# A hybrid decoder layer on one core: the main expert stage written out as a pipeline, and more gathered rows in an earlier stage

## The chip, the cores and the metric

The kernel runs on one core of one Trainium2 chip. The metric is the device time of one execution in microseconds (us), input and output in HBM included. All data are fp32; some of the matrix products take operands of type fp32r, each split in a high part and a remainder.

## The reference

One decoder layer for 512 tokens of width 1024. A token sublayer (retention and forgetting attention, gated and merged) is followed by a channel sublayer, which is what the change is mostly about: a retrieval over 16,384 experts of one neuron each (128 x 128 product keys), plus a gated embedding.

```python
def decoder_layer(x, p):                                   # 512 x 1024
    h = layer_norm(x)
    rq, rk, rv, rg, fq, fk, fv, ff, gr, gf = split(h @ w_in)
    y_ret = (silu(rg) * group_norm(retention(rotary(rq), rotary(rk), rv))) @ w_ret_o
    y_fox = forgetting_attention(fq, fk, fv, log_sigmoid(ff + b_forget)) @ w_fox_o
    merged = sigmoid(gr + b0) * y_ret + sigmoid(gf + b1) * y_fox
    h = layer_norm(ALPHA * h + merged @ w_out)
    ple = sigmoid(h @ w_ple_gate + b) * (p @ w_ple)
    return layer_norm(ALPHA * h + peer(h) + ple)

def peer(h):                                               # 8 heads, 16 experts per token and head
    s, idx = top_k(einsum('nhcd,hckd->nhck', h @ w_q, sub_keys), 16)
    top_s, eid = top_k(all 256 sums of a head's two lists, 16)
    act = gelu(einsum('nhkd,nd->nhk', expert_u[eid], h)) * softmax(top_s)
    return einsum('nhk,nhkd->nd', act, expert_v[eid])
```

## The kernel before

The 512 tokens are two pairs of 128-token blocks, `FIRST` and `REST`. Everything up to the experts is done for `FIRST`, then for `REST`; the experts of the two pairs are computed in two different ways, side by side.

**The first pair's experts are gathered, row by row** (`Gather`). A token has 8 x 16 = 128 experts, and so has a block 128 columns: for one column, `fetch` (L869) issues on POOL an indirect DMA that brings one row of `peer_u` or `peer_v`, 1024 numbers, for each of the 128 tokens into one row buffer. `up` (L875) then multiplies it with the tokens on the DVE, with a sum; `down` (L885) adds it, weighted, to the residual `h0`. A block is 128 ups, one gelu, 128 downs; two blocks make 512 such rows. They wait in a queue, `k.feed.items`. The queue is asked for work by `k.tick`, once for each weight load of a projection, and hands out `rate` items per call, which is set by stage: 1, then 2.25 in `last_blocks` (the second pair's attention and output projections, "the second pair's first stage", 56 weight loads), 0.5 in the second pair's product keys and embedding gate, 0.75 in `spread`. What is left by the main stage is spread evenly over its blocks by `pace`.

**The second pair's experts are computed densely** (`Experts`), all 128 groups ("blocks" of the main stage) of 128 experts each. `up` is the up half of a block: 8 matmuls in the code, 16 in the trace (L799), of a `ur` tile, loaded for two blocks at once, with the tokens `h1`, and a gelu (L801) that gives `a`. `load` takes `vr`, also two blocks at once, and splits it in a high and a low fp32r part, `vh` on ACT (L196) and `vl` on the DVE (L197). `gated` multiplies `a` with the retrieval's gates `gw` on the DVE (L824; `gw` is loaded for four blocks at once) and splits the product in `ah` (ACT) and `al` (DVE). `down` is the down half: 12 matmuls (L837 to L839), `ah`·`vh`, `ah`·`vl` and `al`·`vh` for two token blocks and two halves of the width, summed over all 128 blocks in four PSUM banks `acc`. 40 up halves (`lead`) are done in `spread`, while the gates are scattered into `gd`, and four (`RES`) just ahead of the main stage's first down half, with the banks of `acc` as their target.

**Order.** The kernel is written against a tile scheduler, which places the instructions of every engine by its own timeline. From `spread` on (`in_order`) it does so for PE, ACT and the SP queue alone; DVE and POOL there keep the order in which the program emits them. In the main stage that order is, for each block: load of the next block, an up half, gate and split of the next block, the down half, then `pace` rows. Buffers: two each of `vr`, `vh`, `vl`, `gw`, `ah`, `al` (the pool `dp` has `bufs=2`); the rows go round over 8 buffers (`near`), 4 more in `dp` (`far`) and one in slot `S2`.

`Borrow` lends some tags of the first pair's product keys a place in another pool; three tags share the LG buffers of tag `lg`, `sc` (the scores that leave the PSUM tile `sp`, L642 and L645) among them. Other lines that are named below: L454 the swish product `z`, L530 the retention's product with its branch gate (`sgr`), L475 the residual that ends the second pair's first stage, L217 a weight load (`wr`).

## Time and profile before

| | |
|---|---|
| time, median of 3 runs (lowest to highest) | 1914.91 us (1912.94 to 1918.87) |
| the profiled execution: its time, its span | 1914.95 us, 1913.2 us |
| PE (matmul) busy | 1708.9 us, 89% |
| PE weight loads | 1375.3 us, 72%, beside the matmuls |
| DVE busy | 1362.5 us, 71% |
| POOL busy | 719.0 us, 38% |
| ACT busy | 610.8 us, 32% |
| DMA | 553.92 MB, mean 290 GB/s over the span |

The shares are means over a program with very different parts. In order of time: the first pair's attention and product keys (to about 444 us), the second pair's first stage (to about 752), its product keys, embedding gate and `spread` (to about 1090), the main stage (to about 1863) and the tail. The main stage has two parts: while there are up halves left to do, to about 1649 us, and after that with down halves alone. The DMA row of the page's table by slices shows the same parts: it lies above 300 GB/s from about 430 to 670 us and from 910 to 1815.

### The profile page before, as it was taken

How to read it: one execution, taken by the hardware profiler on the slowest of the kernel's cores; microseconds unless marked ns; L12 is line 12 of the kernel's file. 1: busy time of each engine (PE TensorE's matmuls, PEld its weight loads, DVE VectorE, ACT ScalarE, POOL GpSimd, SP SyncE). 2: the span in 40 equal slices, each digit the busy share in tenths (PEclk: the TensorE clock that was granted, in tenths of full speed). 3: DMA queues.
4: the chain of work that ended last, by engine and by line, in shares of the span. 5: the costliest groups of instructions: out<-in, count | busy, mean ns of one | idle time of the engine just before them, and what ended most of it. 6: DMA issues, size and time to landing. Idle time of an engine off the chain costs nothing.

```text
span 1913.2 us, 22617 instructions
## 1 busy us (share of the span) xinstructions
PE 1708.9 (89%) x7996; PEld 1375.3 (72%) x7996; DVE 1362.5 (71%) x2625; ACT 610.8 (32%) x1130; POOL 719.0 (38%) x523
## 2 busy tenths in 40 slices
PE   6999999997999898999999699999999999766664
PEld 6889888755777474877989588777888878544443
DVE  7543563699877733588979377877877778888885
ACT  4556542121133210114668322232222222222221
POOL 1000000028756720011334355555656555665630
PEclk9999999998999899999999899999999999987887
DMA  7433454459999974565888899999999999999971
GB/s 232 158 122 128 143 191 149 148 206 372 400 322 328 395 282 156 190 209 169 336 331 326 347 380 405 381 370 373 396 398 383 400 387 396 349 347 334 328 258 56
DMA packets 164674, 553.92 MB, mean 290 GB/s; under 512 B 18768, under 2 KB 52560, under 8 KB 147152
## 3 DMA queue, kind: packets, MB, share of 16 engines
q1 hardware_dynamic: 90832, 284.00, 40.9%
q0 software_dynamic: 73728, 268.47, 37.4%
q8 instruction: 63, 1.03, 0.2%
q14 instruction: 51, 0.42, 0.1%
HBM read 533.54 MB, written 18.87 MB: 289 GB/s over the span
## 4 chain that ended last, share of the span: by engine, by line
issue 41%; PE 25%; POOL 15%; DVE 10%; DMA 7%; ACT 2%; SPq 0%; POOLq 0%; DVEq 0%; ACTq 0%
POOL row L869 14%; PE pj L249 10%; PE pj L252 4%; PE hid L799 3%; DMA row<-in_peer_u,geu 3%; DVE h L885 2%; DMA row<-in_peer_v,geu 1%; PE gp L771 1%; DVE oa L762 1%; DVE ob L763 1%; DVE row L875 1%; PE ry L325 1%; PE lg L408 1%; PE sp L642 1%; DMA h<-in_x 1%
## 5 line engine op out<-in xcount | busy, mean ns | idle before, releaser
L869 POOL DMA_INDIRECT row<-in_peer_v,geu x256 | 351.4, 1373 | 509.9 <-DVE h L885 337.5
L869 POOL DMA_INDIRECT row<-in_peer_u,geu x256 | 355.7, 1389 | 329.1 <-DVE row L875 124.4
L799 PE MATMUL hid<-h1f,ur 128*128 128x256 f32 x1984 | 444.0, 380 | 3.7 <-DMA ur<-in_uT 3.7
L799 PEld LDWEIGHTS hid<-h1f,ur 128*128 128x128 f32 x1984 | 375.7, 191 | 57.7 <-DMA ur<-in_uT 3.9
L837 PE MATMUL acc<-vh,ah 128*128 128x512 f32 x512 | 230.0, 449 | 128.6 <-ACT ah L196 124.2
L885 DVE SCALAR_TENSOR_TENSOR h<-row,ghid,h 128x1024 f32<-128x1024 f32 x256 | 328.3, 1282 | 6.4 <-DMA row<-in_peer_v,geu 1.6
L875 DVE SCALAR_TENSOR_TENSOR row<-row,xg 128x1024 f32<-128x1024 f32 x256 | 303.0, 1219 | 20.3 <-DMA row<-in_peer_u,geu 20.1
L837 PEld LDWEIGHTS acc<-vh,ah 128*128 128x128 f32 x512 | 104.7, 205 | 176.5 <-ACT ah L196 150.9
L197 DVE TENSOR_TENSOR vl<-vr,vh 128x1024 fp32r<-128x1024 f32 x128 | 156.2, 1220 | 90.3 <-ACT vh L196 90.2
L838 PE MATMUL acc<-vl,ah 128*128 128x512 f32 x512 | 216.3, 423 | 0.0
L196 ACT ACTIVATE vh<-vr 128x1024 fp32r<-128x1024 f32 x128 | 134.7, 1054 | 173.5 <-PE acc L839 162.3
L839 PE MATMUL acc<-vh,al 128*128 128x512 f32 x512 | 166.1, 409 | 0.0
L190 POOL TENSOR_TENSOR h<-h,b 128x512 f32<-128x512 f32 x7 | 11.7, 1679 | 346.8 <-ACT h L189 346.8
L197 DVE TENSOR_TENSOR wl<-wr,wh 128x1024 fp32r<-128x1024 f32 x72 | 89.6, 1244 | 71.9 <-ACT wh L196 71.7
L196 ACT ACTIVATE ah<-a 128x256 fp32r<-128x256 f32 x128 | 52.9, 413 | 252.5 <-DVE a L824 252.1
L838 PEld LDWEIGHTS acc<-vl,ah 128*128 128x128 f32 x512 | 105.6, 206 | 20.9
L839 PEld LDWEIGHTS acc<-vh,al 128*128 128x128 f32 x512 | 103.0, 201 | 23.3
L197 DVE TENSOR_TENSOR al<-a,ah 128x256 fp32r<-128x256 f32 x128 | 54.5, 426 | 88.3 <-ACT ah L196 88.3
L249 PE MATMUL pj<-hT,wr 128*128 128x256 f32 x512 | 115.3, 380 | 0.0
L249 PE MATMUL pj<-h1f,wr 128*128 128x256 f32 x512 | 113.7, 382 | 0.0
L801 ACT ACTIVATE a<-hid 128x256 f32<-128x256 f32 x124 | 46.8, 380 | 194.0 <-PE hid L799 193.8
L249 PEld LDWEIGHTS pj<-h1f,wr 128*128 128x128 f32 x512 | 97.4, 192 | 13.3 <-ACT h1f L211 0.3
(229 smaller groups left out, 2530.9 us busy)
## 6 DMA issues: line engine op xcount, KB each, us to landing
ur<-in_uT SPq DMA_DIRECT2D x64, 1024.0 KB, 9.2
vr<-in_vP SPq DMA_DIRECT2D x64, 1024.0 KB, 8.3
wr<-in_w_in SPq DMA_DIRECT2D x104, 512.0 KB, 3.9
wr<-in_w_peer_q SPq DMA_DIRECT2D x32, 512.0 KB, 3.3
gd<-stg SPq DMA_DIRECT2D x8, 2048.0 KB, 9.8
gw<-gd SPq DMA_DIRECT2D x32, 512.0 KB, 14.9
wr<-in_w_ret_o SPq DMA_DIRECT2D x16, 512.0 KB, 3.4
wr<-in_w_out SPq DMA_DIRECT2D x16, 512.0 KB, 3.3
```

Of the source, the lines that this page charges most:

```text
L196: k.nc.scalar.activation(hi, src, AF.Copy)
L197: k.nc.vector.tensor_tensor(lo, src, hi.bitcast(F32), op=ALU.subtract)
L249: nc.tensor.matmul(ps[q // 2][:, o:o + G.N], w[:, a, sl], part(x, c), start=first and q % 2 == 0, stop=last, skip_group_check=True)
L252: nc.tensor.matmul(ps[q], part(x, c)[:, sl], w[:, a, :], start=first, stop=last)
L799: nc.tensor.matmul(ps, self.uraw[:, b % 2, c, :], k.h1[:, c, :], start=c == 0, stop=c == 7)
L801: nc.scalar.activation(a, ps, AF.Gelu)
L837: nc.tensor.matmul(acc[m][g], ah[:, sl], vh[:, vs], start=b == 0, stop=False, skip_group_check=True)
L838: nc.tensor.matmul(acc[m][g], ah[:, sl], vl[:, vs], start=False, stop=False, skip_group_check=True)
L839: nc.tensor.matmul(acc[m][g], al[:, sl], vh[:, vs], start=False, stop=b == NK - 1, skip_group_check=True)
L869: k.nc.gpsimd.indirect_dma_start(out=r, out_offset=None, in_=src, in_offset=bass.IndirectOffsetOnAxis(ap=self.e[:, c:c + 1], axis=0))
L875: self.k.nc.vector.scalar_tensor_tensor(r, r, 1.0, self.x, op0=ALU.mult, op1=ALU.mult, accum_out=self.hid[:, c:c + 1])
L885: self.k.nc.vector.scalar_tensor_tensor(h1, r, self.hid[:, c:c + 1], h1, op0=ALU.mult, op1=ALU.add)
```

## The change

Four things are done; some lines have other numbers in the kernel after (`vl` and `al`, L197 before, are L831, `vh` is L811 and `ah` L827; L837 to L839 are L840 to L842, L885 is L888).

1. In `decoder_layer` the rate of the feed in the second pair's first stage is 3.25 items per call for 2.25. The total of 512 rows stays, so the main stage's `pace` falls.
2. The main stage is emitted as a pipeline: the split of V is loaded two blocks ahead and its DVE part, `remainder`, stands apart from its ACT part; the gate runs three blocks ahead, `al` two; the rows of a block are handed out in two halves, between the gate and `vl` and between `vl` and `al`. `vh`, `vl` and `al` have three buffers, `ah` four, `gw` comes with the gate.
3. To make room, the row buffers of the main stage are 11 for 13, and the constants `g2` and `b2` of the last layer norm lie in slot `S2`.
4. `sc` in the first pair's product keys has two buffers of its own.

```diff
@@ class Borrow @@
-    TAGS = {"keys": "lg", "qs": "lg", "sc": "lg", "w": "sm", "cand": "sm"}
+    TAGS = {"keys": "lg", "qs": "lg", "w": "sm", "cand": "sm"}
@@ class Experts, load @@
-        hi = dv.tile([P, D], F32R, tag="vhi", name=k.uniq("vh"))
-        lo = dv.tile([P, D], F32R, tag="vlo", name=k.uniq("vl"))
-        split(k, hi, lo, self.vraw[:, b % 2])
-        self.vw[b] = (hi, lo)
+        hi = dv.tile([P, D], F32R, tag="vhi", bufs=3, name=k.uniq("vh"))
+        lo = dv.tile([P, D], F32R, tag="vlo", bufs=3, name=k.uniq("vl"))
+        nc.scalar.activation(hi, self.vraw[:, b % 2], AF.Copy)
+        self.vw[b] = (hi, lo, self.vraw[:, b % 2])
+
+    def gate(self, b, dp):
...
-    def gated(self, b, dp):
-        k, nc, ND = self.k, self.k.nc, self.ND
-        a = self.act.pop(b)
+        a = self.act[b]
         a3 = a.rearrange("p (g n) -> p g n", n=SG)
         nc.vector.tensor_tensor(a3, a3, self.gw.pop(b), op=ALU.mult)
-        ah = dp.tile([P, ND], F32R, tag="ah", name=k.uniq("ah"))
-        al = dp.tile([P, ND], F32R, tag="al", name=k.uniq("al"))
-        split(k, ah, al, a)
-        self.act[b] = (ah, al)
+        ah = dp.tile([P, ND], F32R, tag="ah", bufs=4, name=k.uniq("ah"))
+        al = dp.tile([P, ND], F32R, tag="al", bufs=3, name=k.uniq("al"))
+        nc.scalar.activation(ah, a, AF.Copy)
+        self.act[b] = (ah, al, a)
+
+    def remainder(self, hi, lo, raw):
+        self.k.nc.vector.tensor_tensor(lo, raw, hi.bitcast(F32), op=ALU.subtract)
@@ channel @@
-    near, far = (k.gp, "row", ROWS), (dp, "row2", 4)
-    k.rows = [near, far, near] * 4 + [(k.cp, "S2", 1)]
-    g2 = dp.tile([P, D], F32, bufs=1, name="g2")
-    b2 = dp.tile([P, D], F32, bufs=1, name="b2")
+    near, far = (k.gp, "row", ROWS), (dp, "row2", 3)
+    k.rows = [near, near, near, far] * 2 + [near, near, far]
+    gb = k.slot([P, 2, D], F32, "S2", "gb2")
+    g2, b2 = gb[:, 0, :], gb[:, 1, :]
...
-    ex.load(0, dp)
+    for b in range(2):
+        ex.load(b, dp)
     for i in range(RES):
         ex.up(lead + i, acc[i // 2][i % 2][:, :ex.ND])
-    ex.gated(0, dp)
+    for b in range(3):
+        ex.gate(b, dp)
+    for b in range(2):
+        ex.remainder(*ex.vw[b])
+        ex.remainder(*ex.act[b])
     for b in range(NK):
-        if b + 1 < NK:
-            ex.load(b + 1, dp)
+        if b + 2 < NK:
+            ex.load(b + 2, dp)
         if b + lead + RES < NK:
             ex.up(b + lead + RES)
-        if b + 1 < NK:
-            ex.gated(b + 1, dp)
+        if b + 3 < NK:
+            ex.gate(b + 3, dp)
+        k.feed(pace / 2)
+        if b + 2 < NK:
+            ex.remainder(*ex.vw[b + 2])
+        k.feed(pace / 2)
+        if b + 2 < NK:
+            ex.remainder(*ex.act[b + 2])
         if b < NK - 2:
             ex.down(b, acc, range(len(dense)))
...
-        k.feed(pace)
@@ decoder_layer @@
-        k.feed.rate = 2.25
+        k.feed.rate = 3.25
         last_blocks(k, act, rq)
```

The order of instructions shows the moves. The first place is the DVE in the last part of the main stage (down halves alone). A row of the order is the line, the operation, output and inputs with their tile numbers, and the output's shape; `L885` and `L888` are gathered rows. Before:

```order
L197 TENSOR_TENSOR vl_11260<-vr_11257,vh_11259 128x1024
L824 TENSOR_TENSOR a_9514<-a_9514,gw_11202 128x256
L197 TENSOR_TENSOR al_11265<-a_9514,ah_11264 128x256
L885 SCALAR_TENSOR_TENSOR h_65<-row_11280,ghid_2765,h_65 128x1024
L885 SCALAR_TENSOR_TENSOR h_65<-row_11283,ghid_2765,h_65 128x1024
L197 TENSOR_TENSOR vl_11287<-vr_11257,vh_11286 128x1024
L824 TENSOR_TENSOR a_9559<-a_9559,gw_11202 128x256
L197 TENSOR_TENSOR al_11292<-a_9559,ah_11291 128x256
```

And after:

```order
L888 SCALAR_TENSOR_TENSOR h_65<-row_11296,ghid_2765,h_65 128x1024
L831 TENSOR_TENSOR vl_11290<-vr_11287,vh_11289 128x1024
L888 SCALAR_TENSOR_TENSOR h_65<-row_11300,ghid_2765,h_65 128x1024
L831 TENSOR_TENSOR al_11265<-a_9634,ah_11264 128x256
L824 TENSOR_TENSOR a_9714<-a_9714,gw_11319 128x256
L888 SCALAR_TENSOR_TENSOR h_65<-row_11325,ghid_2765,h_65 128x1024
L831 TENSOR_TENSOR vl_11317<-vr_11287,vh_11316 128x1024
L888 SCALAR_TENSOR_TENSOR h_65<-row_11329,ghid_2765,h_65 128x1024
L831 TENSOR_TENSOR al_11294<-a_9672,ah_11293 128x256
L824 TENSOR_TENSOR a_9752<-a_9752,gw_11319 128x256
```

Before, a block was vl, gate, al, and then its two or three rows one behind the other, and all three operations served the block that came next. After, rows stand between them, and `al` (of `a_9634`) belongs to the last gate but one.

On ACT, in the same part, the splits before:

```order
L196 ACTIVATE ah_11232<-a_9471 128x256
L196 ACTIVATE vh_11259<-vr_11257 128x1024
L196 ACTIVATE vh_11286<-vr_11257 128x1024
L196 ACTIVATE ah_11264<-a_9514 128x256
L196 ACTIVATE ah_11291<-a_9559 128x256
L196 ACTIVATE vh_11318<-vr_11316 128x1024
L196 ACTIVATE vh_11350<-vr_11316 128x1024
```

And after:

```order
L827 ACTIVATE ah_11264<-a_9634 128x256
L827 ACTIVATE ah_11293<-a_9672 128x256
L811 ACTIVATE vh_11289<-vr_11287 128x1024
L811 ACTIVATE vh_11316<-vr_11287 128x1024
L827 ACTIVATE ah_11322<-a_9714 128x256
L827 ACTIVATE ah_11351<-a_9752 128x256
L811 ACTIVATE vh_11347<-vr_11345 128x1024
```

The pairs of `vh` and of `ah` take turns in both; after, the two `ah` belong to blocks further ahead than the two `vh` that follow them.

The second place is the DVE at the end of the second pair's first stage. `sgf` and `sgr` are evacuations of a projection's PSUM tiles `pj`, L475 (`h_65<-h_65,pj`) the residual behind the last projection. Before:

```order
L539 TENSOR_TENSOR sgf_741_4058<-pj_4963,sgf_741_4058 128x512
L540 TENSOR_TENSOR sgr_4057<-sgr_4057,sgf_741_4058 128x512
L539 TENSOR_TENSOR sgf_742_4059<-pj_5000,sgf_742_4059 128x512
L540 TENSOR_TENSOR sgr_4057<-sgr_4057,sgf_742_4059 128x512
L539 TENSOR_TENSOR sgf_742_4059<-pj_5001,sgf_742_4059 128x512
L540 TENSOR_TENSOR sgr_4057<-sgr_4057,sgf_742_4059 128x512
L475 SCALAR_TENSOR_TENSOR h_65<-h_65,pj_5047 128x512
L166 BN_STATS st_5045<-h_65 128x6
```

And after:

```order
L888 SCALAR_TENSOR_TENSOR h_65<-row_5243,ghid_2748,h_65 128x1024
L888 SCALAR_TENSOR_TENSOR h_65<-row_5246,ghid_2748,h_65 128x1024
L888 SCALAR_TENSOR_TENSOR h_65<-row_5249,ghid_2748,h_65 128x1024
L539 TENSOR_TENSOR sgf_754_4095<-pj_5137,sgf_754_4095 128x512
L539 TENSOR_TENSOR sgf_754_4095<-pj_5138,sgf_754_4095 128x512
L888 SCALAR_TENSOR_TENSOR h_65<-row_5252,ghid_2748,h_65 128x1024
L540 TENSOR_TENSOR sgr_4093<-sgr_4093,sgf_754_4095 128x512 x2
L888 SCALAR_TENSOR_TENSOR h_65<-row_5267,ghid_2748,h_65 128x1024
L888 SCALAR_TENSOR_TENSOR h_65<-row_5270,ghid_2748,h_65 128x1024
L888 SCALAR_TENSOR_TENSOR h_65<-row_5273,ghid_2748,h_65 128x1024
```

Before, no row stood among these evacuations; after, rows stand between and behind them.

The third place is PE at the start of the main stage, from the last scatter matmul (L771) to the first down matmul. Before:

```order
L771 MATMUL gp_7439<-oa_7409,ob_7410 128x128 x4
L799 MATMUL acc_0_7474<-h1f,ur_7490 128x256 x8
L799 MATMUL acc_1_7475<-h1f,ur_7490 128x256 x8
L799 MATMUL acc_0_7476<-h1f,ur_7512 128x256 x8
L799 MATMUL acc_1_7477<-h1f,ur_7512 128x256 x8
L837 MATMUL acc_0_7474<-vh_7484,ah_7535 128x512
```

And after:

```order
L771 MATMUL gp_7607<-oa_7577,ob_7578 128x128 x4
L799 MATMUL acc_0_7642<-h1f,ur_7657 128x256 x8
L799 MATMUL acc_1_7643<-h1f,ur_7657 128x256 x8
L799 MATMUL acc_0_7644<-h1f,ur_7679 128x256 x8
L799 MATMUL acc_1_7645<-h1f,ur_7679 128x256 x8
L799 MATMUL hid_7726<-h1f,ur_7724 128x256 x8
L799 MATMUL hid_7764<-h1f,ur_7724 128x256 x8
L840 MATMUL acc_0_7642<-vh_7651,ah_7704 128x512
```

Two more up halves (`hid`) now stand ahead of the first down half.

## Rows read from the trace of the kernel before

**Rows 1.** The profile's page: its first line, and part 1 (busy time of each engine, share of the span, instructions).

```profile
span 1913.2 us, 22617 instructions
...
PE 1708.9 (89%) x7996; PEld 1375.3 (72%) x7996; DVE 1362.5 (71%) x2625; ACT 610.8 (32%) x1130; POOL 719.0 (38%) x523
```

**Rows 2.** Busy time by stretch. A row is one stretch in us from the span's start: its length, then busy us and (x instructions) of PE, PE weight loads, DVE, ACT and POOL, then the granted TensorE clock, the mean busy share of the 16 DMA engines and GB/s.

```profile
416.00:660.00 244.00, 222.39 (x923) 156.21 (x922) 188.77 (x405) 56.79 (x106) 174.35 (x130) 0.97 0.97 359
660.00:680.00 20.00, 17.22 (x55) 9.57 (x54) 19.10 (x25) 6.24 (x10) 15.46 (x14) 0.81 1.03 409
680.00:750.00 70.00, 68.72 (x262) 48.75 (x260) 13.42 (x19) 2.87 (x5) 3.85 (x3) 1.00 0.54 192
...
1090.00:1649.00 559.00, 534.51 (x2376) 449.71 (x2376) 428.90 (x617) 153.23 (x259) 307.89 (x217) 0.99 1.01 386
1649.00:1863.00 214.00, 136.05 (x432) 97.91 (x432) 188.12 (x207) 52.68 (x73) 117.61 (x85) 0.84 0.90 325
```

**Rows 3.** The PE in order of time in a full block of the main stage: start us, length us, what, xcount. Matmuls overlap, so the cost of one is the distance between starts.

```profile
1405.99 0.39 PE L839 MATMUL acc<-vh,al 128*128 128x512 f32 x1
...
1408.04 0.39 PE L839 MATMUL acc<-vh,al 128*128 128x512 f32 x1
...
1412.79 4.48 PE L799 MATMUL hid<-h1f,ur 128*128 128x256 f32 x20
```

**Rows 4.** Who waited for whom: engine and line, what it waited for, us in total, times, longest. The first three rows are of 1090 to 1649 us, the last is of 1649 to 1863.

```profile
PE acc L837 <- ACT ah L196: 38.0, 19, 13.8
...
DVE vl L197 <- ACT vh L196: 67.4, 26, 6.3
...
ACT vh L196 <- PE acc L839: 66.3, 42, 2.4
...
PE acc L837 <- ACT ah L196: 72.4, 33, 3.3
```

**Rows 5.** DVE and ACT in order of time in one block of the last part; in brackets the idle time before and what ended it.

```profile
1701.54 1.22 DVE L197 TENSOR_TENSOR vl<-vr,vh 128x1024 fp32r<-128x1024 f32 x1
1702.67 0.42 DVE L824 TENSOR_TENSOR a<-a,gw 128x256 f32<-128x256 f32 x1
...
1703.51 1.04 ACT L196 ACTIVATE vh<-vr 128x1024 fp32r<-128x1024 f32 x1
1703.63 0.43 DVE L197 TENSOR_TENSOR al<-a,ah 128x256 fp32r<-128x256 f32 x1 [0.54 <-ACT ah L196]
...
1703.97 2.60 DVE L885 SCALAR_TENSOR_TENSOR h<-row,ghid,h 128x1024 f32<-128x1024 f32 x2
...
1706.49 1.22 DVE L197 TENSOR_TENSOR vl<-vr,vh 128x1024 fp32r<-128x1024 f32 x1
```

**Rows 6.** Of 1649 to 1863 us: the group of row operations on the DVE (xcount | busy us, mean ns | idle before), and the vl operations (xcount: ns min/median/max, first and last start).

```profile
L885 DVE SCALAR_TENSOR_TENSOR h<-row,ghid,h 128x1024 f32<-128x1024 f32 x94 | 120.5, 1282 | 2.1
...
L197 DVE TENSOR_TENSOR vl<-vr,vh x37: 1215/1218/1220, 1648.8 to 1863.0; 128x1024 fp32r<-128x1024 f32 x37
```

**Rows 7.** DMA issues (xcount, KB each, median us to landing), and the time to landing of all row gathers.

```profile
ur<-in_uT SPq DMA_DIRECT2D x64, 1024.0 KB, 9.2
vr<-in_vP SPq DMA_DIRECT2D x64, 1024.0 KB, 8.3
...
gw<-gd SPq DMA_DIRECT2D x32, 512.0 KB, 14.9
...
DMA to landing us min/median/max: 4.1/8.8/16.6
```

**Rows 8.** The DVE in order of time at the end of the second pair's first stage (its second swish product z, and its last two residuals), and the loads of w_ret_o issued from 664 to 680 us.

```profile
677.59 1.29 DVE L454 TENSOR_TENSOR z<-z,si 128x512 f32<-128x512 f32 x2
...
750.46 0.69 DVE L475 SCALAR_TENSOR_TENSOR h<-h,pj 128x512 f32<-128x512 f32 x1 [11.00 <-PE pj L252]
...
752.50 0.69 DVE L166 BATCH_NORM_STATS2 st<-h 128x6 f32<-128x512 f32 x1
...
L217 SPq DMA_DIRECT2D wr<-in_w_ret_o x3: 327/327/328, 669.5 to 676.3; - x3
```

**Rows 9.** Row gathers (L869) by stretch: length, POOL's busy us and (x gathers), then clock, DMA share and GB/s. The two rows are of two answers.

```profile
416.00:660.00 244.00, 174.35 (x130) 0.97 0.97 359
...
1090.00:1649.00 559.00, 307.89 (x217) 0.99 1.01 386
```

**Rows 10.** The start of the main stage in order of time.

```profile
1089.36 0.42 DVE L824 TENSOR_TENSOR a<-a,gw 128x256 f32<-128x256 f32 x1 [8.91 <-DMA gw<-gd]
...
1090.29 0.80 PE L837 MATMUL acc<-vh,ah 128*128 128x512 f32 x1 [13.81 <-ACT ah L196]
...
1090.88 0.63 PE L838 MATMUL acc<-vl,ah 128*128 128x512 f32 x1
...
1091.31 0.63 PE L837 MATMUL acc<-vh,ah 128*128 128x512 f32 x1
```

**Rows 11.** ACT in order of time at the end of the first pair's product keys, and PE's wait between 440 and 460 us.

```profile
369.65 0.60 ACT L645 ACTIVATE sc<-sp 128x512 f32<-128x512 f32 x1 [7.96 <-PE sp L642]
...
377.78 0.58 ACT L645 ACTIVATE sc<-sp 128x512 f32<-128x512 f32 x1
...
PE pf L357 <- DVE w L731: 10.3, 1, 10.3
```

More of the change, by code (lines that the diff above doesn't have):

```diff
@@ L808, in load @@
             nc.sync.dma_start(self.vraw, k.I["vP"][b // 2])
-        hi = dv.tile([P, D], F32R, tag="vhi", name=k.uniq("vh"))
-        lo = dv.tile([P, D], F32R, tag="vlo", name=k.uniq("vl"))
-        split(k, hi, lo, self.vraw[:, b % 2])
-        self.vw[b] = (hi, lo)
+        hi = dv.tile([P, D], F32R, tag="vhi", bufs=3, name=k.uniq("vh"))
[3 more added lines that the diff above has]
+    def gate(self, b, dp):
+        k, nc, ND = self.k, self.k.nc, self.ND
         if b % 4 == 0:
-            g = dv.tile([P, self.ND // SG, 4, SG], F32, tag="gw", name=k.uniq("gw"))
+            g = dp.tile([P, ND // SG, 4, SG], F32, tag="gw", name=k.uniq("gw"))
             nc.sync.dma_start(g.rearrange("p g i n -> p g (i n)"),
@@ L818, in load @@
                 self.gw[b + i] = g[:, :, i, :]
-    def gated(self, b, dp):
-        k, nc, ND = self.k, self.k.nc, self.ND
-        a = self.act.pop(b)
+        a = self.act[b]
         a3 = a.rearrange("p (g n) -> p g n", n=SG)
         nc.vector.tensor_tensor(a3, a3, self.gw.pop(b), op=ALU.mult)
-        ah = dp.tile([P, ND], F32R, tag="ah", name=k.uniq("ah"))
-        al = dp.tile([P, ND], F32R, tag="al", name=k.uniq("al"))
-        split(k, ah, al, a)
-        self.act[b] = (ah, al)
+        ah = dp.tile([P, ND], F32R, tag="ah", bufs=4, name=k.uniq("ah"))
[4 more added lines that the diff above has]
+        self.k.nc.vector.tensor_tensor(lo, raw, hi.bitcast(F32), op=ALU.subtract)
     def down(self, b, acc, ms):
         nc = self.k.nc
-        (ah, al), (vh, vl) = self.act[b], self.vw[b]
+        (ah, al, _), (vh, vl, _) = self.act[b], self.vw[b]
         for m in ms:
```

## The prediction

> **What bounds the kernel now.** I first took the stretches [rows 2]. From 1090 to 1649 us (main stage, blocks that still have an up half; "first part" below) the PE is busy 534.51 of 559 us and the DMA engines stand at a share of 1.01 with 386 GB/s; from 1649 to 1863 (down halves alone; "last part") the PE falls to 136.05 of 214 and the DVE, at 188.12, is the fullest.
>
> Busy PE overlaps pipelined matmuls, so I counted start to start [rows 3]: nine down matmuls from 1405.99 to 1408.04 are 0.228 us each; twenty up matmuls take 4.48 us, or 0.215 each without the last one's own 0.39. A down half is 12 x 0.228 = 2.74 us, an up half 16 x 0.215 = 3.45, a full block 6.19. The 84 full blocks (128 less 40 led and 4 preset) and one down half need 523 of the 559 us. Of the 36 lost, 24.2 are named: 38.0 us of waits for ah, less the 13.8 before the first block [rows 4, 10]. Behind them the views show a ring: gate stands behind vl on the DVE, vl waited 67.4 us for vh, and vh 66.3 us for the PE to leave the old vh [rows 4].
>
> In the last part the PE waits 72.4 us for ah [rows 4]. A two-row block on the DVE, from 1701.54 to 1706.49 [rows 5], is 4.95 us: vl 1.13, gate 0.42, a wait of 0.54 for ACT's ah, al 0.34, rows 1.32 + 1.20. With 94 rows on 36 steps from 1648.8 to 1863.0 [rows 6] a block takes 5.95 us: the DVE sets it.
>
> Last, bytes. A row is 128 x 4 KB = 0.524 MB; u and v are 1024 KB for two blocks each, gw 512 KB for four [rows 7]. With 217 rows in the first part [rows 9] a block moves 2.53 MB, 6.55 us at 386 GB/s, against 559/84.5 = 6.6 us. So the first part is bounded by transfers and PE alike, and a better order without fewer rows would win little there.
>
> **Part by part.** The sum is made on the profiled execution, 1914.95 us with a span of 1913.2 [rows 1]; the median of the three runs, 1914.91, is the same.
>
> *More rows early.* The feed is asked once per weight load, 56 times in this stage: one more each time is 56 rows, and the order has 254 rows ahead of the first vl instead of 198. The scheduler puts almost all of them behind the second z: 143 rows done there instead of 136, but 195 instead of 139 at the first residual. Before, that tail was PE's: z at 677.59, the last residuals from 750.46, done at 752.5 [rows 8], DMA at 0.54 [rows 2]. Now 52 rows lie in it, and each evacuation of a projection waits on the DVE behind some of them. I put the z at 683 (7 more rows, which start some 4 us earlier, below). From there some 48 rows and 17 to 20 weight loads of the same 0.524 MB must still move (8 rows are in the buffers, half of the 8 after row 195 ride along, 3 loads were issued by 676 [rows 8]): 65 to 68 transfers, 1.28 us each at the 409 GB/s of 660 to 680, 1.46 at the 359 GB/s of 416 to 660 [rows 2]. That is 83 to 99 us, 766 to 782, and 4 us of residuals: +18 to +34. I take **+24**, near the fast end, since the tail is nothing but such traffic; bounds +14 (z not late) to +40 (z at 691).
>
> *sc with buffers of its own.* The second sp of each key group moves ahead of the next projection. The last sc was copied at 377.78, 8 us after its twin at 369.65, and the chain from there ends in 10.3 us of PE waiting for the forget weights' memset [rows 11]. The DVE gains some 4 us, but PE now reaches that wait one weight load (3.45 us) earlier in its work: **-2**, bounds -4 and +2.
>
> *Start of the main stage.* Gate 0 waited for gw until 1089.36 [rows 10]; ur for blocks 44 and 45 is now issued ahead of vr and gw, so gw lands up to 2.5 us later (1 MB at 409 GB/s), and three gates of 0.42 stand ahead of the first vl: **+3.5**, bounds 0 and +6.
>
> *First part.* Two up halves (6.9 us) move into the 13.8 us in which the PE stood [rows 10]. The ring opens: gates run three blocks ahead, vh and vl have three buffers, ah four. A block now moves 2.14 rows (261 items over 122 blocks), 2.29 MB, 5.9 us at 386 GB/s: under the PE's 6.19. The DVE needs 4.5 (next term). So 523 - 6.9 = 516, plus the 12 us of loss that the waits do not explain, 528: **-31**. Bounds: -38 (half of the 12 goes too) and -15 (half of the waits stay, and 4 us of late transfers come).
>
> *Last part.* DVE per block: 1.13 + 0.42 + 0.34 + 2.14 x 1.20, since rows no longer follow each other: 4.46. ACT now makes two ah before two vh, so every second vl waits for ah (0.54) and vh (1.05) while the DVE has one row of 1.20 to do: 0.4 a pair, 4.66 a block. Transfers, 1.78 MB: 4.35 us at 409 GB/s, 4.6 at 386, 4.9 at the 325/0.90 = 361 of this stretch. Two limits this close disturb each other; I take 4.85 x 36.5 = 177: **-37**. Bounds: 4.5 (-50) and 5.3 (-21), for a PE at 1.2 GHz, half its clock, needs 12 x 0.43 = 5.1 [rows 10], and the granted clock here was 0.84 [rows 2].
>
> Two row buffers fewer (11 for 13) cost nothing while a row lands in 8.8 us, 16.6 at most [rows 7]: 11 rows are 24 us of work at 4.85 a block. SP's order keeps vr three blocks ahead, 14.5 us, as before; if transfers crowd, vr is the first to be late, and that lies in the 4.85. The tail after 1863 keeps its work.
>
> Sum: 24 - 2 + 3.5 - 31 - 37 = -42.5, **1872 us**. All terms at their good ends give 1841, all at their bad ends 1927.
>
> **Rivals.** *Transfers at the lower rate.* If 386 and 409 GB/s are not to be had with this mix, but 359 as from 416 to 660 [rows 2], a block of the first part takes 2.29/0.359 = 6.38 us and 84.5 of them 539 (-20), one of the last part 4.96 (-33), and the row stage is at +34: 1914.95 - 2 + 34 + 3.5 - 20 - 33 = 1897. For it: the last part ran at 325 GB/s. Against it: 386 over 559 us. The Trainium skill, "DMA: Bandwidth & Descriptors", section "Bandwidth", puts the HBM side's limit for one core at about 358 GB/s and says that it binds transfers between HBM and SBUF; by that rule the time would be this 1897. The trace disagrees, with 386 and 409 GB/s.
>
> *The handoffs stay.* ACT takes its work in order, and a gate that is late holds the ah, then the pair of vh and the gelu behind it. If half of the waits stay, -15 and -21 in place of -31 and -37: 1904. For it: ACT waited 66.3 us for the PE in the first part already. Against it: the DVE has 1.7 us to spare in each full block.
>
> *Both limits are reached.* Row stage +14, first part -38, last part -50, start 0: 1839. For it: both had 4.5 us of work.
>
> *The row stage gives it all back* (slower). Eight buffers serve the tail; a row holds one through issue, landing and the DVE's turn, and the PE's evacuations queue behind it. From 416 to 660 a row took 244/130 = 1.88 us [rows 9], loads included, and 52 of them are 98 us, within my bounds. At 2.6 us a row the tail ends at 822, +66 in all, and the rest is eaten; at 2.9, 838 and +85: 1933. For it: landings of up to 16.6 us [rows 7] would make 16.6/8 = 2.1 plus the turn on the DVE.
>
> That the change does nothing is not open: the order shows the rows and the two up halves moved.
>
> **Chances.** Forecast 0.58 (1850 to 1894), lower transfer rate 0.10, handoffs stay 0.12, both limits 0.12, row stage gives it back 0.08. The range, 1845 to 1903, holds the first two and half each of the next two. Within 0.3% (5.7 us) is what a measurement of this kernel cannot tell from no change. Faster: forecast, both limits, and most of the two at 1897 and 1904, which have 12 and 5 us to spare: 0.82. Same: the rest of those two, 0.08. Slower: the row stage and an accident of the same kind in the order, 0.10.
>
> **What would show it.** Row stage: last residual near 776 instead of 750.46, DMA near 1.0 from 680 on, 200 row issues by then instead of 147; PE waiting for DVE rows. Start: up halves just ahead of the first down. First part: DMA below 1.0, no DVE wait for vh, PE waits of a few us; 82 up blocks in some 528 us. Last part: blocks of 4.7 to 5.0 us, rows and vl alternating, DMA at 0.95 or more. It would be wrong if the tail's rows come at 2.6 us or more, if the PE still waits 1.5 us for ah every fourth block, or if DVE rows begin to wait for their landing in the main stage.

## The result, and the profile after

The kernel after takes 1862.09 us (median of 4 runs, 1854.51 to 1864.67) against 1916.87 for the kernel before (4 runs, 1912.94 to 1918.87): a ratio of 0.971, interval 0.9677 to 0.9744, or 55 us less. The prediction was 1872 us, 1845 to 1903, and faster. The profiled execution of after is its fastest run, 1854.51 us; the other three took 1861.62 to 1864.67, so the differences of traces below add up to 60.5 us and not to 55. One execution of an experiment below, rows in one piece, ran at a granted clock of 0.62 and took 2956 us; it is left out of that experiment's figures, and as it is the profiled one, no block time is given there.

The page of after, first line and part 1:

```profile
span 1852.7 us, 22582 instructions
...
PE 1698.6 (92%) x7996; PEld 1358.1 (73%) x7996; DVE 1349.3 (73%) x2625; ACT 608.4 (33%) x1130; POOL 662.9 (36%) x523
```

Busy time by stretch in after, columns as in [rows 2]. The stretches are the second pair's first stage up to its second z and from there to its last residual, the first part, and the last part as far as it has rows:

```profile
413.00:692.00 279.00, 245.61 (x966) 167.53 (x964) 213.18 (x426) 61.04 (x112) 193.89 (x150) 0.93 0.96 357
692.00:786.00 94.00, 78.51 (x276) 53.13 (x276) 78.64 (x73) 4.27 (x6) 64.75 (x54) 0.92 1.02 404
1120.00:1636.00 516.00, 514.59 (x2314) 438.22 (x2315) 367.69 (x570) 149.36 (x256) 211.72 (x174) 1.00 0.98 372
1640.00:1814.00 174.00, 131.68 (x461) 84.83 (x460) 168.43 (x199) 53.84 (x78) 90.75 (x71) 0.94 0.95 360
```

In the first part PE is busy for 514.59 of 516 us; before it was 534.51 of 559 [rows 2]. In the last part the DVE is busy for 168.43 of 174, 97%, against 188.12 of 214. The row tail of the second pair's first stage, 692 to 786, is now full of transfers: 404 GB/s at a DMA share of 1.02, where before it was 192 at 0.54 [rows 2].

Who waited for whom on PE in after, first from 1120 to 1636 us, then from 1640 to 1815; the last row is the DVE's of that second stretch:

```profile
PE acc L840 <- ACT ah L827: 6.5, 1, 6.5
PE acc L842 <- DVE al L831: 0.8, 3, 0.3
PE acc L840 <- ACT vh L811: 0.5, 1, 0.5
...
PE acc L842 <- DVE al L831: 12.7, 30, 1.6
PE acc L841 <- DVE vl L831: 12.4, 19, 1.9
PE acc L840 <- ACT vh L811: 8.8, 12, 2.1
PE acc L840 <- DVE acc L969: 8.3, 1, 8.3
...
DVE vl L831 <- ACT vh L811: 5.4, 14, 1.3
```

The 38.0 us of PE waiting for ah in the first part [rows 4] are one wait of 6.5, at the start; the 72.4 of the last part are gone. In their place stand 33.9 us of short waits for al, vl and vh, none over 2.1 us, and one of 8.3 for the DVE's addition of the residual to `acc` (4.4 before).

The DVE in a pair of blocks of after's last part:

```profile
1796.52 1.21 DVE L831 TENSOR_TENSOR vl<-vr,vh 128x1024 fp32r<-128x1024 f32 x1
1797.65 1.27 DVE L888 SCALAR_TENSOR_TENSOR h<-row,ghid,h 128x1024 f32<-128x1024 f32 x1
1798.85 0.41 DVE L831 TENSOR_TENSOR al<-a,ah 128x256 fp32r<-128x256 f32 x1
1799.18 0.41 DVE L824 TENSOR_TENSOR a<-a,gw 128x256 f32<-128x256 f32 x1
1799.52 1.27 DVE L888 SCALAR_TENSOR_TENSOR h<-row,ghid,h 128x1024 f32<-128x1024 f32 x1
1801.09 1.22 DVE L831 TENSOR_TENSOR vl<-vr,vh 128x1024 fp32r<-128x1024 f32 x1 [0.30 <-ACT vh L811]
...
1805.29 1.22 DVE L831 TENSOR_TENSOR vl<-vr,vh 128x1024 fp32r<-128x1024 f32 x1
```

The two blocks take 4.57 and 4.20 us; of the waits of [rows 5] 0.30 in one of the two is left (over the stretch 5.4 us, in 14 waits). Over the last part a block takes 4.63 us (38 from 1637.9 to 1813.7), before 5.92.

Where the time went, from marks in the traces: the start of the last residual, the start of the first down half, the end of the last up half, the end of the last down half. The columns of the two kernels between (next section) stand beside them.

| us | before | rows alone | pipeline alone | after |
|---|---|---|---|---|
| start to last residual | 751.8 | 784.9 | 756.3 | 785.7 |
| to first down half | 338.5 | 337.0 | 340.9 | 334.2 |
| to end of last up half | 549.2 | 533.3 | 544.0 | 515.8 |
| to end of last down half | 257.4 | 236.1 | 227.7 | 200.7 |
| to the end | 16.3 | 16.3 | 16.3 | 16.3 |
| span | 1913.2 | 1907.6 | 1885.2 | 1852.7 |

### The profile page after: what moved, and what is told of

Read it like the earlier page. It is cut to its first block, busy times and chain, and to the rows that moved or that the text cites. A ratio compares the mean times of both kernels' runs of the same rounds, so it can differ in the third digit from the quotient of the medians.

```text
span 1852.7 us, 22582 instructions
## 1 busy us (share of the span) xinstructions
PE 1698.6 (92%) x7996; PEld 1358.1 (73%) x7996; DVE 1349.3 (73%) x2625; ACT 608.4 (33%) x1130; POOL 662.9 (36%) x523
## 3 DMA queue, kind: packets, MB, share of 16 engines
q1 hardware_dynamic: 90832, 284.00, 42.5%
## 4 chain that ended last, share of the span: by engine, by line
PE 48%; issue 21%; DVE 15%; DMA 10%; POOL 3%; ACT 2%; SPq 0%; DVEq 0%; ACTq 0%; POOLq 0%
PE hid L799 18%; PE pj L249 9%; DVE h L888 5%; PE acc L842 4%; PE acc L840 4%; PE acc L841 4%; DMA row<-in_peer_v,geu 3%; PE pj L252 3%; DMA row<-in_peer_u,geu 3%; POOL row L872 2%; PE gp L771 1%; DVE row L878 1%; DVE oa L762 1%; ACT vh L811 1%; DVE ob L763 1%
## 5 line engine op out<-in xcount | busy, mean ns | idle before, releaser
L872 POOL DMA_INDIRECT row<-in_peer_v,geu x256 | 333.6, 1303 | 410.4 <-DVE h L888 269.4
L872 POOL DMA_INDIRECT row<-in_peer_u,geu x256 | 317.4, 1240 | 437.9 <-DVE row L878 221.1
L888 DVE SCALAR_TENSOR_TENSOR h<-row,ghid,h 128x1024 f32<-128x1024 f32 x256 | 328.0, 1281 | 18.6 <-DMA row<-in_peer_v,geu 16.4
L831 DVE TENSOR_TENSOR vl<-vr,vh 128x1024 fp32r<-128x1024 f32 x128 | 156.3, 1221 | 154.6 <-ACT vh L811 154.6
L842 PE MATMUL acc<-vh,al 128*128 128x512 f32 x512 | 159.4, 413 | 19.8 <-DVE al L831 19.8
L841 PE MATMUL acc<-vl,ah 128*128 128x512 f32 x512 | 159.5, 412 | 13.1 <-DVE vl L831 12.4
L840 PE MATMUL acc<-vh,ah 128*128 128x512 f32 x512 | 146.2, 405 | 24.1 <-ACT vh L811 9.3
L827 ACT ACTIVATE ah<-a 128x256 fp32r<-128x256 f32 x128 | 53.3, 418 | 315.7 <-DVE a L824 305.9
L197 DVE TENSOR_TENSOR wl<-wr,wh 128x1024 fp32r<-128x1024 f32 x72 | 89.4, 1242 | 72.2 <-ACT wh L196 71.9
L840 PEld LDWEIGHTS acc<-vh,ah 128*128 128x128 f32 x512 | 97.7, 193 | 50.8 <-ACT vh L811 14.9
L842 PEld LDWEIGHTS acc<-vh,al 128*128 128x128 f32 x512 | 95.8, 193 | 52.9 <-DVE al L831 35.1
L811 ACT ACTIVATE vh<-vr 128x1024 fp32r<-128x1024 f32 x128 | 128.2, 1047 | 16.2 <-DMA vr<-in_vP 10.4
L841 PEld LDWEIGHTS acc<-vl,ah 128*128 128x128 f32 x512 | 95.7, 192 | 46.0 <-DVE vl L831 27.7
L801 ACT ACTIVATE a<-hid 128x256 f32<-128x256 f32 x124 | 47.1, 380 | 200.8 <-PE hid L799 200.7
L249 PEld LDWEIGHTS pj<-hT,wr 128*128 128x128 f32 x512 | 97.4, 192 | 15.5 <-DVE sg L666 1.6
```

Source lines behind the costliest of these rows:

```text
L197: k.nc.vector.tensor_tensor(lo, src, hi.bitcast(F32), op=ALU.subtract)
L249: nc.tensor.matmul(ps[q // 2][:, o:o + G.N], w[:, a, sl], part(x, c), start=first and q % 2 == 0, stop=last, skip_group_check=True)
L811: nc.scalar.activation(hi, self.vraw[:, b % 2], AF.Copy)
L831: self.k.nc.vector.tensor_tensor(lo, raw, hi.bitcast(F32), op=ALU.subtract)
L840: nc.tensor.matmul(acc[m][g], ah[:, sl], vh[:, vs], start=b == 0, stop=False, skip_group_check=True)
L841: nc.tensor.matmul(acc[m][g], ah[:, sl], vl[:, vs], start=False, stop=False, skip_group_check=True)
```

## The experiments

### Pipeline alone, rows alone

Theory A was that the pipeline takes the handoffs away and that transfers then set the pace. The first kernel undoes the rows, the second has nothing but the rows.

```diff
 # pipeline alone: the kernel after
-        k.feed.rate = 3.25
+        k.feed.rate = 2.25
 # rows alone: the kernel before
-        k.feed.rate = 2.25
+        k.feed.rate = 3.25
```

> The kernel after, with the feed's rate in the second pair's first stage put back to 2.25: the pipeline and sc alone, 198 rows ahead of the main stage. Theory A (the pipeline removes the handoffs, and then transfers set the pace of a block with 2.6 rows): the second pair's first stage loses its extra, so the last residual starts near 747; first part 2.53 MB a block at 386 GB/s, 6.55 us, some 540 us from first down half to last up half (549 before, 516 after); last part 5.3 us a block (2.02 MB at 386 GB/s), tail 11 us shorter as in the kernel after: about 1867 us, so that pipeline and rows together are worth little more than the pipeline. Rival B (the pipeline alone takes the first part to the PE's pace, rows or no rows): first part 516, 1842 us, faster than after. Rival C (the fewer rows do the work): 1900 us or more.

> The kernel before, with the feed's rate in the second pair's first stage at 3.25: more rows early, no pipeline, 254 rows ahead of the main stage. Theory A: the stage ends 34 us later; first part 5.9 us of transfers a block, but the waits for ah and vh stay, some 535 us; last part 5.95 less 0.47 rows of 1.26, 5.36 us a block, -22 us; tail as before: 1910 to 1918 us, no gain without the pipeline. Rival C (fewer rows do the work): 1870 to 1880 us.

Measured: pipeline alone 1893.13 us, ratio 0.9886 (0.9869 to 0.9902); rows alone 1911.83, 0.9976 (0.9958 to 0.9993). Apart they are worth 22 and 5 us, together 55. The rows alone came out as theory A had them (1910 to 1918 us). Busy time by stretch in the pipeline alone (its first and last part), and then in the rows alone:

```profile
1097.00:1641.00 544.00, 525.02 (x2313) 435.35 (x2313) 411.48 (x607) 147.22 (x254) 287.00 (x212) 1.00 1.00 386
1645.00:1846.00 201.00, 141.93 (x462) 93.11 (x462) 195.73 (x221) 53.40 (x78) 121.00 (x91) 0.89 0.96 361
```

```profile
1122.00:1655.00 533.00, 523.85 (x2352) 445.16 (x2352) 375.87 (x569) 149.62 (x255) 251.89 (x175) 1.00 0.97 366
1660.00:1858.00 198.00, 135.15 (x441) 97.22 (x442) 169.25 (x193) 52.37 (x74) 101.19 (x69) 0.86 0.86 309
```

With the pipeline alone the first part stands at 386 GB/s and a DMA share of 1.00, as before the change, and from one up half to the next it takes 6.53 us, before 6.50: nothing is won inside the blocks, because 2.6 rows a block do not come any faster. That part of theory A held (540 us expected, 544 measured). But the waits are not removed, as it had it. PE's waits in the first part, in the pipeline alone (1097 to 1641 us) and then in the rows alone (1122 to 1655 us; its first row only):

```profile
PE acc L842 <- DVE al L831: 12.2, 16, 1.7
PE acc L840 <- ACT ah L827: 7.6, 1, 7.6
PE acc L840 <- ACT vh L811: 3.0, 6, 0.5
PE acc L841 <- DVE vl L831: 3.0, 6, 0.6
```

```profile
PE acc L837 <- ACT ah L196: 21.4, 8, 13.6
```

Behind the first block that is 18.2 us with the pipeline alone, now for al, vl and vh, and 7.8 for ah with the rows alone; before, it was 24.2 [rows 4, 10]. So most of these waits went with the number of rows and not with the order.

With the pipeline alone the DVE is busy 97% of the last part, at 5.22 us a block. Theory A's total, 1867, did not hold. In the profiled execution, which is the fastest of the four, its terms miss by 21 us: the second pair's first stage is 4.5 us later and not 5 earlier (9.5), the last part and the blocks behind it give 30 for 35, the first part 5 for 9, the way to the first down half is 2.4 longer; the other runs lie 5 to 10 us higher still. So its claim that the rows add little fell: on top of the pipeline they are worth 31 us by the medians, 33 by the ratios. Rivals B (1842) and C (1900) fell as well.

With the rows alone the first part goes nearly at PE's pace, 6.30 us from one up half to the next (6.19 in after). What is left to the pipeline there is the two up halves ahead of it and the 7.8 us of waits. In the last part the old handoffs stay; PE's wait in the rows alone, from 1660 to 1858 us:

```profile
PE acc L837 <- ACT ah L196: 61.6, 35, 3.3
```

So in the first part the two are worth more together because each alone leaves the other's limit standing, at nearly the same height: full transfers in the one, the waits in the other. By the table the traces give 27 us more for both than for each by itself, added: 12 of them in the first part, 6 behind it and 9 ahead of the first down half, where a single trace can't tell as much (see sc below). The rows' price in the second pair's first stage, 33 us without the pipeline and 29 with it, is paid either way.

### What holds the last part: half the DVE work, half the bytes, both

```diff
 # half the DVE work: also in Gather.down
+        q = slice(0, D // 2)
-        self.k.nc.vector.scalar_tensor_tensor(r, r, 1.0, self.x, ...
+        self.k.nc.vector.scalar_tensor_tensor(r[:, q], r[:, q], 1.0, self.x[:, q], ...
 # half the bytes: the operation reads the half twice
-        self.k.nc.gpsimd.indirect_dma_start(out=r, out_offset=None, in_=src,
+        self.k.nc.gpsimd.indirect_dma_start(out=r[:, D // 2:], out_offset=None,
+                                       in_=src.rearrange("e (h d) -> (e h) d", h=2),
```

> The kernel after, with the DVE's operation on a gathered row cut to its first 512 numbers (the rows are fetched whole; half of the gathered experts' arithmetic is left out). Theory A (the second pair's first stage is bounded by transfers, the last part by DVE and transfers at nearly the same size): last residual within 6 us of 785.7, first part 510 to 516 us, last part 4.4 to 4.6 us a block. Rival (the DVE's turn bounds both): last residual 20 us or more earlier, last part 3.4 to 3.8 us a block.

> The kernel after, with only 2 KB fetched for each gathered row in place of 4 (the operation on the DVE keeps its width and takes the half twice; the gathered experts' sums are therefore wrong). Theory A: the second pair's first stage, bounded by transfers, ends 25 us or more earlier; first part still 510 to 518 us (PE); last part still 4.4 to 4.6 us a block (the DVE). Rival (it is the landing of each row, not its bytes, that counts): last residual within 8 us of 785.7.

> The kernel after, with 2 KB fetched for each gathered row and the DVE's operation at half its width. Theory A (two limits of about the same height in the last part, so that taking one away alone gives nothing): last part 3.3 to 3.7 us a block, which neither half_dve nor half_bytes reaches; first part 505 to 515 us. Rival (a ring of handoffs between ACT, DVE and PE sets the last part): 4.4 us or more.

Busy time of the last part, as far as it has rows, with half the DVE work, with half the bytes, and with both; each from its own kernel, of which there is one execution each (a row's operation `h<-row` on the DVE takes 746 ns at half width, 1280 in after):

```profile
1645.00:1805.00 160.00, 118.22 (x431) 81.05 (x430) 118.58 (x188) 51.04 (x73) 76.06 (x68) 0.89 0.97 370
```

```profile
1677.00:1842.00 165.00, 126.19 (x457) 84.52 (x456) 162.95 (x193) 54.84 (x75) 97.90 (x69) 0.95 0.74 253
```

```profile
1617.00:1746.00 129.00, 116.91 (x457) 82.13 (x456) 121.35 (x194) 50.63 (x73) 83.13 (x69) 0.97 0.90 325
```

A block takes 4.50 us, 4.51 and 3.53 (4.63 in after). Taking either load away alone gives 0.1 us, both together 1.1. With half the DVE work the transfers are full (0.97) and the DVE has time (118.58 of 160); with half the bytes it is the other way round (0.74; 162.95 of 165). This is the theory's picture of two limits at the same height, and the rival, a ring of handoffs, falls.

The second pair's first stage told less. With half the DVE work its last residual starts at 784.4 us for 785.7: the DVE's work doesn't set it, which fits theory A. With half the bytes it starts at 825.0, later, but there the scheduler moved the rows: 203 gathers were issued ahead of the second z in place of 150, 50 ahead of the pair's forget matmul in place of 22, and that matmul already comes 48 us later (497.2 us for 448.7), so that kernel does not test that stage. With both, also 203 ahead of z but 24 ahead of the forget matmul, the last residual starts at 767.1. And with half the DVE work the last up half comes later (1642.0 us for 1635.7) with blocks of the same 6.1 to 6.3 us; PE's order had changed (84 up halves behind the first down half for 82, and more of the down halves), which the expectation of 510 to 516 us (528 measured) had not taken in. With both halves it is 520 us for 505 to 515 expected, also with 84.

### The place of the rows, and the third V buffer

```diff
 # rows in one piece behind al
-        k.feed(pace / 2)
         if b + 2 < NK:
             ex.remainder(*ex.vw[b + 2])
-        k.feed(pace / 2)
...
+        k.feed(pace)
 # two V buffers
-        hi = dv.tile([P, D], F32R, tag="vhi", bufs=3, ...
-        lo = dv.tile([P, D], F32R, tag="vlo", bufs=3, ...
+        hi = dv.tile([P, D], F32R, tag="vhi", bufs=2, ...
+        lo = dv.tile([P, D], F32R, tag="vlo", bufs=2, ...
```

> The kernel after, with a block's rows handed out in one piece behind al, as before the change, all else as in the pipeline. Theory A (the blocks of lookahead and the buffers carry the gain, the place of the rows little): within 6 us of the kernel after, 1858 to 1868 us. Rival (the rows between gate, vl and al are what hides the waits for vh and ah): last part 5.0 to 5.3 us a block, 1877 to 1890 us.

> The kernel after with two buffers each for vh and vl in place of three; the order in which the program emits the work is untouched. Theory A (the lookahead carries the pipeline's gain, and it needs the third buffer: with two, vl of the next block but one waits until PE has left the block that runs now): last part 5.2 us a block or more for 4.63, first part 525 to 540 us for 516: 1885 to 1905 us, near the kernel without the pipeline. Rival (the order alone carries it): within 6 us of the kernel after.

Rows in one piece: 1867.85 to 1875.99 us in four executions, ratio 0.9741 (0.9706 to 0.9775). Two buffers: 1866.83, 0.9742 (0.9717 to 0.9768). Both are about 0.3% from after's 0.971 with intervals that overlap it: neither piece carries the pipeline's gain. The rows in one piece are nearer to theory A than to its rival, though mostly above the 1868 us that it allowed; of the second pair of theories the rival was right (order, not the buffer; with two buffers a block of the last part takes 4.72 us, where 5.2 were expected). What remains by exclusion is the lookahead in the order, gates three blocks ahead and al two; it was not undone by itself.

### sc

```diff
 # sc alone: the kernel before. Without sc: the kernel after, the other way round
-    TAGS = {"keys": "lg", "qs": "lg", "sc": "lg", "w": "sm", "cand": "sm"}
+    TAGS = {"keys": "lg", "qs": "lg", "w": "sm", "cand": "sm"}
```

> The kernel before with sc in two buffers of its own and nothing else. If the 5.5 us by which the kernel after reaches the second pair's forget matmul earlier are sc's and are kept to the end: 1910 us. Rival: something later takes them back, 1915 us.

> The kernel after with sc back in the shared LG buffers. If sc is worth the 5.5 us by which the kernel after reaches the second pair's forget matmul earlier: 1867 us. Rival (the earlier start is spent in the stage behind it, where 7 fewer rows stand ahead of the second z without sc's change, 136 for 143, and transfers set the end): within 4 us of the kernel after, and the last residual within 5 us of 785.7.

sc alone: 1921.5 us, 1.0016 (1.0 to 1.0032). After without sc: 1864.07, 0.9713 (0.9688 to 0.9737). Its gain at the front is there (the last of the second pair's forget matmuls starts 2.9 us earlier in the one, and 5.5 later again without sc in the other) but not at the end. Without sc the second z comes at 682.2 us, with it at 692.3, and the last residual at 786.4 and 785.7: the seven rows ahead of that z only change places with rows behind it. As for sc alone, one execution says little. The DVE's z operations in the pipeline alone and in sc alone, two kernels whose instructions are the same up to the last residual (xcount: ns min/median/max, first and last start):

```profile
L454 DVE TENSOR_TENSOR z<-z,si x8: 683/686/694, 204.7 to 684.3; 128x512 f32<-128x512 f32 x8
```

```profile
L454 DVE TENSOR_TENSOR z<-z,si x8: 682/692/694, 204.6 to 691.5; 128x512 f32<-128x512 f32 x8
```

The same work ends 7 us apart, and its last residual 8 (756.3 and 764.6 us). A term of a few microseconds in this stage can't be read from one trace.

### Where else the rows could go

```diff
 # uneven: keys2 has 0.85 for 0.8; its low form has 0.8
-    pace = len(k.feed.items) / (NK - 6)
+    total = len(k.feed.items)
+    late = 0.8 * total / (NK - 6)
+    early = (total - 40 * late) / (NK - 46)
...
+        pace = early if b < NK - 46 else late
 # keys2, and its low form with 2.75 for 3.25 in last_blocks
-            k.feed.rate = 0.5
+            k.feed.rate = 1.5
             s16, i16 = product_keys(k, REST, rp, kp, k.h1)
...
+            k.feed.rate = 0.75
             embedding_gate(k, REST, k.h1, ...
```

> The kernel after, with its main stage's rows handed out unevenly: 0.8 of the even pace in the last 40 blocks that get rows (1.71 a block), the rest in the first 82 (2.35), in place of 2.14 in both. Theory A (the first part is held by PE, the last by the DVE's 1.13 + 0.42 + 0.34 + 2.14 x 1.20 us): first part longer by at most 5 us (2.4 MB a block at 386 GB/s is 6.2 us), last part 3.95 to 4.2 us a block for 4.63, -16 to -25 us: about 1846 us. Rival (the first part is at the limit of its transfers too, 369 GB/s at a DMA share of 0.98): 6.2 us a block become 6.5, +24 us, and the sum is nothing: 1862 to 1867 us.

> The kernel after with more rows in the second pair's product keys (rate 1.5 for 0.5, 0.75 in its embedding gate), where the DMA engines are busy at 0.58 to 0.71 and the DVE has idle time: 272 rows ahead of the main stage for 254; and 0.85 of the even pace in its last 40 blocks with rows. A block has 2.1 rows in the first part, as in the kernel after, and 1.7 in the last, as in the uneven one. Theory: first part 516 to 520 us, last part 4.1 us a block, the main stage's start 0 to 6 us later: 1843 to 1852 us. Rival (the DVE's top-k operations behind those rows come late and hold the gates): start 10 us or more later, 1856 us or more.

> As keys2, with the rate in the second pair's first stage at 2.75 for 3.25 and 0.8 of the even pace in the last 40 blocks: 244 rows ahead of the main stage, 171 for 199 at the last residual. Theory: that stage ends 14 us earlier than in the kernel after; a block of the first part has 2.4 rows and 2.4 MB, at 372 GB/s 6.5 us, 533 us for 516; last part 4.15 us a block: 1845 to 1852 us, the same as keys2. Rival (the stage gives back less than 8 us): 1856 us.

Uneven: 1855.33 us, ratio 0.965 (0.9617 to 0.9683), between the two theories. Its first and last part:

```profile
1128.00:1660.00 532.00, 523.57 (x2319) 437.69 (x2320) 387.91 (x588) 149.34 (x257) 252.99 (x191) 0.99 1.00 377
1662.00:1814.00 152.00, 123.24 (x450) 80.99 (x449) 145.11 (x178) 52.30 (x75) 75.89 (x55) 0.97 0.94 351
```

The last part falls to 4.13 us a block, as theory A had it, but the first goes to 6.37 from one up half to the next (532 us for 516) at a DMA share of 1.00: with 2.35 rows a block it is bounded by transfers again. So the kernel after has PE and transfers at the same height there too.

keys2: 1851.04 us, 0.9639 (0.9606 to 0.9673), the lowest median of a version with all the work, though its interval overlaps that of uneven. The rows did not go where they were meant to go first. From its last residual on, 34 us (786 to 820 in after, 795 to 829 in keys2), the DVE has as little to do as in after; the rows stand in the 131 us behind, 28 gathers for 17 (in each pair the first row is of after, the second of keys2):

```profile
786.00:820.00 34.00, 27.83 (x136) 24.93 (x137) 7.60 (x25) 4.59 (x9) 0.00 (x0) 0.90 0.71 259
...
795.00:829.00 34.00, 27.69 (x129) 24.59 (x130) 7.73 (x24) 3.99 (x8) 0.62 (x1) 0.83 0.71 252
```

```profile
820.00:951.00 131.00, 131.00 (x586) 101.80 (x586) 116.49 (x425) 41.21 (x86) 21.22 (x17) 1.00 0.59 197
...
829.00:960.00 131.00, 131.00 (x570) 101.16 (x570) 120.49 (x410) 33.44 (x62) 32.09 (x28) 1.00 0.69 245
```

Its main stage starts 10 us later than after's (1129.7 for 1119.9), as much as the rival said, but 9 of these stand already at the last residual (794.8 for 785.7), ahead of the rival's top-k operations. From there the gates' scatter ends another 10 us later, where the rival's delay may lie, and the first down half follows it 9 us sooner, with two up halves fewer ahead of it. Its first part takes 526 us, a block of its last part 4.21; only the median lies where the theory had it, and the profiled execution, the slowest of its four, does not show where its gain comes from. The low form, 1864.10 us, 0.9712 (0.9685 to 0.9739) for 1845 to 1852 expected, gave its 8.4 us in the second pair's first stage back in 11 us more to the first down half, a first part of 538 us and a last part of 4.38 us a block: rows taken out of the early stage come back as transfers later.

## Why the prediction was right, point by point

| term | forecast | traces |
|---|---|---|
| rows early, with sc | +24 - 2 | +33.9 |
| start | +3.5 | -4.3 |
| first part | -31 | -33.4 |
| last part, blocks with rows | -37 | -45.5 |
| blocks behind the last row | 0 | -11.2 |
| sum | -42.5 | -60.5 (medians -55) |

The forecast of 1872 us is 10 above the median. Part of that nearness is luck: the early rows cost 12 us more than forecast, and a term that the sum did not have gave 11 back. Of the signs that were named, most came: 203 gathers by the last residual, a DMA share of 1.02 in the tail and 0.98 in the first part, rows and vl in turn. Three did not: the last residual starts at 785.7 us for 776, a block of the last part takes 4.63 for 4.7 to 5.0, and the DVE still waits for vh in the first part (below).

**Rows early.** The mechanism was right: the tail behind the second z became all transfers. The size was off. The DVE at the end of the stage in after, as [rows 8]:

```profile
691.70 1.29 DVE L454 TENSOR_TENSOR z<-z,si 128x512 f32<-128x512 f32 x2
...
784.35 0.67 DVE L475 SCALAR_TENSOR_TENSOR h<-h,pj 128x512 f32<-128x512 f32 x1
785.67 0.67 DVE L475 SCALAR_TENSOR_TENSOR h<-h,pj 128x512 f32<-128x512 f32 x1
```

From z to the last residual it is 94 us, inside the 83 to 99 that were worked out. The step that failed is the one ahead: z at 683. Seven rows were priced at 1.35 us (9.4), while the 150 gathers up to z took 1.86 us each with their weight loads (279 us), so that 13 was due; the rest is the scatter of 7 us shown above. Nor was it needed to know z. In the six traces in which 203 gathers of whole rows are issued by then (after, without sc, rows alone, half the DVE work, two buffers, uneven) the last residual starts at 784.4 to 789.6 us, while z lies anywhere from 678.8 to 696.8: that end goes with the number of transfers and hardly with z's place among them.

**sc** is worth nothing that can be measured at the end, for -2 in the forecast. That the start it wins goes into the same transfers is argued from those 203 gathers, not shown by itself.

**Start.** From the last residual to the first down half after is 4.3 us shorter. Of that, 3.7 lie in the scatter of the gates (163.4 and 159.7 us from its first to its last matmul), which the change doesn't touch and which takes 158 to 165 us in the other traces with all the work; from its last matmul to the first down half it is 29.3 us in both. The start in after:

```profile
1106.21 7.17 PE L799 MATMUL hid<-h1f,ur 128*128 128x256 f32 x32
...
1118.96 1.10 DVE L824 TENSOR_TENSOR a<-a,gw 128x256 f32<-128x256 f32 x3 [28.16 <-DMA gw<-gd]
...
1119.89 2.07 PE L840 MATMUL acc<-vh,ah 128*128 128x512 f32 x4 [6.50 <-ACT ah L827]
```

The two up halves lie in the old hole, as forecast (6.50 us of wait for 13.81 in [rows 10]). The 3.5 us for a later gw and three gates did not come: the first down half needs only the first gate's ah, and gw was not later.

**First part.** -33.4 for -31: transfers are down to 372 GB/s at a share of 0.98, and PE's waits behind the first are 1.3 us, as forecast. Two things in the account were off. The 559 us that it started from [rows 2] reach 9.5 us past the end of the last up half: cut there, 549.2 us hold 520 of work (84 x 6.19) and the 24.2 of waits, so that 5 and not 12 stood without a reason. And DVE waits for vh did not go away (DVE and ACT in after, 1120 to 1636 us):

```profile
DVE vl L831 <- ACT vh L811: 147.5, 41, 8.3
...
ACT vh L811 <- PE acc L842: 2.1, 3, 1.1
```

Before, they were 67.4 and 66.3 [rows 4]. So vh no longer waits for PE, which was the ring's link, but vl waits longer for vh; the DVE, busy for 367.69 of 516 us here, has the time, and PE is not held by it. The rows alone already give -15.9 of the term and the pipeline alone -5.2, of which the two up halves are 6.9; the handoffs were the smaller of the two limits.

**Last part.** -45.5 for -37. The term was sized for 4.85 us a block because two limits that close were thought to disturb each other; measured are 4.63. Half the DVE work (4.50, transfers full) and half the bytes (4.51, DVE full) show that both limits stood where the sum put them, 4.46 to 4.66 for the DVE and 4.35 to 4.9 for transfers, with hardly any disturbance.

**The blocks behind the last row** were taken as unchanged and are 11 us shorter (33.9 and 22.7 us from the last vl with rows to the last down half). PE's waits there, before (from 1863 us) and after (from 1814 us):

```profile
PE acc L837 <- ACT ah L196: 13.8, 4, 8.5
```

```profile
PE acc L842 <- DVE al L831: 6.2, 1, 6.2
```

Before, the first pair's last layer norm on the DVE held the next block's gate, ah and al; after, it holds one al, and the four blocks behind it run without a hole. That is 7 of the 11 us (13.8 before; 6.8 after, with a short one of 0.6 for vl), and it is the pipeline's: 22.7 us with the pipeline alone, 33.3 with the rows alone. Most of the rest is the mark: from that vl on PE has 72 down matmuls to go before and 58 after, since vl now runs two blocks ahead. The forecast stopped at the last part's end; this term was missing from the sum.

**The rivals.** Transfers at the lower rate (1897) fell: 404 GB/s in the row tail, 386 GB/s over 544 us with the pipeline alone. The Trainium skill, "DMA: Bandwidth & Descriptors", section "Bandwidth", gives about 358 GB/s as the HBM side's limit for one core; these traces disagree with that as a limit for a core that runs alone, and the same section adds that each core gets about as much when both cores of a pair stream. The handoffs that stay (1904) fell by the waits above. Both limits reached (1839) was closest to what the main stage did. The row stage that gives it all back fell: 54 gathers in 94 us, loads included, are 1.74 us each, not 2.6. Two sums beside the forecast were off: all terms at their good ends give 1837 and not 1841, and a tail that ends at 822 us is +70 and not +66; neither changes the forecast.

## What to carry to other kernels

Where two limits stand at nearly the same height, an experiment on either alone says that it is worth nothing; price both together, and ask of each which one holds when the other is gone. In a stage that is all transfers, count the transfers to its end and leave the order inside it alone. And follow a pipelined loop to its very last block: what a lookahead gives behind the last long operation belongs in the sum.

## What the runs showed of the hardware

The issue of a gathered row on POOL is not of one length. The gathers of the last part, in after and with half the DVE work (xcount: ns min/median/max, first and last start):

```profile
L872 POOL DMA_INDIRECT row<-in_peer_v,geu x71: 932/1212/1862, 1640.6 to 1792.3; - x71
```

```profile
L872 POOL DMA_INDIRECT row<-in_peer_v,geu x69: 933/1032/1672, 1642.1 to 1786.8; - x69
```

The shortest are the same, 932 and 933 ns; the median falls from 1212 to 1032 when the DVE's operations on rows take 746 ns for 1280. The bytes of a row do not count here: in the last part it is 1230 with half the bytes and 1034 with both halves. The Trainium skill, "GPSIMD Engine Reference", section "Specifications", names SBUF interfaces that GpSimd shares with VectorE instructions of two SBUF inputs, as these are; that this is the cause was not tested here.
